# A hybrid decoder block on one NeuronCore: group-norm spread by a diagonal tile, row sums on 64 columns, one gate projection drawn forward, and a changed ending

## Chip, cores and metric

The kernel runs on one core of a Trainium2 chip. The metric is device time in microseconds (us) of one execution. PE is TensorE (PEld its weight loads), DVE VectorE, ACT ScalarE, POOL GpSimd, SP the engine that issues the DMAs.

## What is computed

One decoder block on a sequence of 1024 tokens and 1024 channels, in float32:

```python
h = modulate(rmsnorm(x, norm1_g), shift1, scale1)
u, v, val, gate = split(h @ w_in + b_in)                 # 512 channels each
y_a = gelu(u) * (causal_spatial(layernorm(gelu(v))) + b_s)   # 8 heads, chunks of 128 tokens
y_b = silu(groupnorm(conv31(val * sigmoid(gate)) + conv_b))  # 8 groups of 64 channels
x = x + gate1 * (concat(rmsnorm(y_a), rmsnorm(y_b)) @ w_out)
h2 = modulate(rmsnorm(x, norm2_g), shift2, scale2)
g, up = split(h2 @ w_ffn_in)                             # 2816 channels each
x = x + gate2 * ((silu(g) * up) @ w_ffn_out)
out = modulate(rmsnorm(x, norm_f_g), shift_f, scale_f)
```

The shifts, scales and gates are `silu(c) @ ada_w`, one vector each.

## The kernel before

Channels lie on partitions, tokens on the free axis; the 1024 tokens are worked as two halves of 512 (`half` 0 and 1). Each float32 product is made of three fp32r matmuls, 128x128 weights on 128x512 data: the data and the weights are each split into a rounded part (`wh_`, or the first plane of a tile, made by ACT) and the remainder (`wl_`, or the second plane, made by POOL or DVE), and `mm3` (L682 to L684) sums high*high, low*high, high*low in PSUM. In the feed-forward part the same is line 1073.

The stages stand in the program like this: first norm; value and gate projections `vg_proj` (`p` banks), which end in `glu` (ACT sigmoid, one DVE operation) and write `ypad`; `u_proj` (`pu`); `spatial_bias`; `v_proj` (`v`); the 31-tap convolution `conv`, almost all of it DVE operations on `cv` tiles (L1006); `group_norm`; `spatial` (`pm`); the norms of the two branches (`rstd`, `branch_out`), giving `y_a` and `y_b`; `w_out` (`po`); then the second norm, and the feed-forward part, of which the first quarter (`ah`) is interleaved with half 1 of the mixer. Raw weights come through a ring of four 128x1024 slots (`N_RAW = 4`, the tag "raw"), and so do the 64 columns of the conditioning matrix (`ada`), which DVE or POOL and ACT reduce in the background.

`group_norm` (L1021) works on a pair of 128-channel tiles. Two float32 matmuls with a centring matrix take the mean away (L1026); ACT squares; matmuls with 32 columns of weights collect the squares of both tiles in one 128x128 block, in which 32 partitions stand for one run of 128 tokens (L1033); ACT takes the root and DVE the reciprocal, `gsd` (L1036, L1037). Then the reciprocals are spread over all 128 partitions and 512 tokens. Half 1 (names `g10`, `g11` in `DIAGONAL`) does it by `diagonal` (L614): ACT rounds `gsd` to a high part `low`, four DVE operations on 32 partitions each (L620) write high or remainder into a 128x512 tile, block-diagonally and zero elsewhere, and one matmul per 128-channel tile with a 0/1 matrix `picks` spreads it (L1042). The tile is called `late`, and is made once, by `load_late`, after half 0 is done. Half 0 does it by blocks: 16 float32 matmuls per pair-half, 64 weight columns on 128x128 data, each a 0/1 column of `colt` (L1046). The norms of the branches have the same two ways (L733, L737).

`spatial_bias` (L786) sums the rows of the spatial weights `wt` of four heads at a time, by a float32 matmul of 128 equal columns (L789), and adds them to `bst` in eight DVE operations on 64 partitions (L794).

The last norm is worked in three pieces of the tokens (512, 256, 256). Sums of squares are matmuls with one column of data (L1345, bank `ssq_nf`); ACT and DVE give `rt_nf` (L1374, L1375); matmuls with the identity `eye` spread it (L1377); for each of eight tiles DVE multiplies (L1399), ACT adds the shift (L1401), and SP stores two tiles of 256 tokens at a time (L1403).

The order of the instructions is not that of the code: `fix_order` (L499) schedules the whole program on a list of modelled durations, forward and backward, and fixes each engine's order. Any edit can therefore move instructions on every engine.

Of the kernel before, what the change touches and what calls it, by code (L numbers as in the profile page):

```python
# [7 lines left out]
F32 = mybir.dt.float32  # L8
# [3 lines left out]
ALU = mybir.AluOpType  # L12
# [23 lines left out]
IDLE = (1, 1, 2, 3, 3)  # L36
BEFORE_LAST = ((3, 6), (2, 4), (3, 7), (3, 2))
# [11 lines left out]
    ("sel_grp", 16), ("low_rows", 1), ("sel_hl", 1),  # L49
# [466 lines left out]
def block_kernel(ctx: ExitStack, tc: tile.TileContext, xT, c, ada, cols, vbias, bs, wsp,  # L516
# [21 lines left out]
    def mm_bank(name):  # L538
        return ps.tile([P, 512], F32, tag="mm", name=name)
# [74 lines left out]
    def diagonal(src):  # L614

        diag, low = late["diag"], late["low"]
        A.activation(low, src, AF.Copy)
        for q in range(4):
            rows = slice(32 * q, 32 * q + 32)
            V.scalar_tensor_tensor(diag[rows, q * P:(q + 1) * P], low[rows].bitcast(F32), col("low_rows")[rows], src[rows],  # L620
                                   op0=ALU.mult, op1=ALU.add)
        return diag
# [163 lines left out]
    def spatial_bias():  # L786
        for q in range(2):
            rs = mm_bank(f"rs{q}")
            PE.matmul(rs, ones.broadcast_to([P, P]), wt[:, 4 * q:4 * q + 4, :], start=True, stop=True)  # L789
            for hh in range(4):  # L790
                hd = 4 * q + hh
                e, hp = hd % 2, hd // 2
                rows = slice(e * 64, (e + 1) * 64)
                V.scalar_tensor_tensor(bst[rows, hp, :], rs[rows, hh * P:(hh + 1) * P],  # L794
                                       col("a_ln_b", hp)[rows], bst[rows, hp, :],
                                       op0=ALU.mult, op1=ALU.add)
# [224 lines left out]
    def group_norm(half, jp, js, s):  # L1021
# [17 lines left out]
        both = sd if by_block else diagonal(sd)  # L1039
        for i, (j, b) in enumerate(zip(js, (b1, b0))):  # L1040
            if not by_block:
                PE.matmul(b, late["picks"][:, i * P:(i + 1) * P], both, start=True, stop=True)  # L1042
            for q in range(4):
                for g in range(2):
                    if by_block:
                        PE.matmul(b[g * 64:(g + 1) * 64, q * P:(q + 1) * P],  # L1046
                                  col("sel_grp", 8 * i + 2 * q + g).broadcast_to([P, 64]), sd,
                                  start=True, stop=True)
            V.tensor_tensor(s[j], s[j], b, op=ALU.mult)
            A.activation(s[j], s[j], AF.Silu, bias=col("b_gn_b", j), scale=col("b_gn_g", j))  # L1050
# [55 lines left out]
    background += [lambda i=i: ada_cols(SHIFT2 * 8 + i, pool=i < 12) for i in range(16)]  # L1106
    v_proj(0)
# [8 lines left out]
    vg_proj(1, (0, 1, 2))  # L1116
# [222 lines left out]
    sums, squares_in, norm_banks = {}, [0, 0, 0], {}  # L1339

    def to_partitions(i, t):

        part = pieces[i]
        for q in range((part.stop - part.start) // P):
            PE.matmul(norm_banks[i][:, q:q + 1], t[:, q * P:(q + 1) * P], ones,  # L1345
                      start=squares_in[i] == q == 0, stop=False, skip_group_check=True)
        squares_in[i] += 1
# [22 lines left out]
    def norm(i):  # L1370
        bank, part = norm_banks[i], pieces[i]
        nq = (part.stop - part.start) // P
# [7 lines left out]
    def output(i, tiles=range(KD), by_pool=()):  # L1380
# [6 lines left out]
        for k in tiles:  # L1387
# [10 lines left out]
            else:  # L1398
                V.scalar_tensor_tensor(t, x_tile(k, part), ccol(SCALEF, k), bank[:, 0:size],  # L1399
                                       op0=ALU.mult, op1=ALU.mult)  # L1400
                A.activation(t, t, AF.Identity, bias=ccol(SHIFTF, k))  # L1401
            if (k + 1) % per_store == 0:
                nc.sync.dma_start(out[(0, KD, KD + KD // 2)[i] + k // per_store], row)  # L1403
# [72 lines left out]
    with issue_after(last_ins):  # L1476
# [5 lines left out]
        norm_banks[1], norm_banks[2] = gn_bank("ssq_nf1"), mm_bank("ssq_nf2")  # L1482
        for i in (1, 2):
# [96 lines left out]
```

## Time and profile before

| | us |
|---|---|
| median of 3 runs (range) | 967.76 (966.22 to 967.87) |
| the profiled execution | 967.97 |
| its span, from first to last instruction | 965.9 |
| PE busy | 950.5 |
| DVE busy | 871.7 |
| ACT busy | 474.0 |
| POOL busy | 408.6 |

Rows of the timeline read: start, length, engine, line, operation, output<-inputs, weights' shape, form of the data, count; in brackets the idle time before them and what ended it. A float32 matmul leaves two or more records. Rows by tile read: shortest/median/longest in ns, first and last start. Rows by stretch give the length, then the busy time of PE, PEld, DVE, ACT and POOL, the granted TensorE clock (1.00 is full), and the DMA share and rate. Neighbouring matmuls overlap, so what one costs is read from start to start.

### The profile page before, as it was taken

Reading aid. Unit: us, or ns where it says so; the run is one execution under the profiler, and the core shown is the slowest. Engines: PE = TensorE matmul, PEld = TensorE weight load, DVE = VectorE, ACT = ScalarE, POOL = GpSimd, SP = SyncE. Lnnn points to the kernel's source line nnn. Section 1 sums busy time; section 2 is a strip of 40 time slices with the busy share of each in tenths; the row PEclk is TensorE's granted clock in tenths of the full one; section 3 lists DMA queues with packets and bytes.
Section 4 is the critical chain, followed back from the end, with each engine's and each line's share of the span. In section 5 each row is a group of like instructions: output and inputs, shape, how many; then the busy total and the mean of one; then the engine's idle time right before and its main releaser. Section 6 shows DMA issues by size and latency. Waiting matters only on the chain.

```text
span 965.9 us, 12960 instructions
## 1 busy us (share of the span) xinstructions
PE 950.5 (98%) x4521; PEld 769.6 (80%) x4521; DVE 871.7 (90%) x1236; ACT 474.0 (49%) x756; POOL 408.6 (42%) x241
## 2 busy tenths in 40 slices
PE   8999999999999999999999999999999999999996
PEld 4887777778777778788888888888888888888885
DVE  6999999999999763999999999999879999969956
ACT  5787477643474753564333333333337437227426
POOL 0089988836453413665444444455433100000132
PEclk9999999999999999999999999999999999999998
DMA  9882542343485444844677678867657857415104
GB/s 353 323 310 91 176 152 69 113 174 131 137 282 188 158 136 146 271 173 147 215 245 239 230 237 261 268 211 257 211 177 264 266 172 258 162 33 159 61 1 174
DMA packets 70498, 184.24 MB, mean 191 GB/s; under 512 B 7841, under 2 KB 8353, under 8 KB 70434
## 3 DMA queue, kind: packets, MB, share of 16 engines
q1 hardware_dynamic: 70434, 183.43, 56.5%
q8 instruction: 35, 0.57, 0.2%
q14 instruction: 29, 0.24, 0.1%
HBM read 142.24 MB, written 41.16 MB: 190 GB/s over the span
## 4 chain that ended last, share of the span: by engine, by line
PE 79%; DVE 15%; ACT 2%; DMA 2%; issue 1%; SPq 0%; ACTq 0%; DVEq 0%
PE B L1073 30%; PE C L1073 18%; PE ah L1073 10%; DVE cv L1006 5%; PE A L1073 3%; PE v L682 2%; PE v L684 2%; PE po L682 2%; PE po L684 2%; PE v L683 2%; PE po L683 2%; PE p L684 1%; PE p L683 1%; PE p L682 1%; DVE ada L636 1%
## 5 line engine op out<-in xcount | busy, mean ns | idle before, releaser
L1073 PE MATMUL B<-h,w_f 128*128 128x512 f32 x816 | 189.6, 389 | 0.1
L1073 PEld LDWEIGHTS B<-h,w_f 128*128 128x128 f32 x816 | 153.0, 188 | 32.5 <-ACT x L1291 0.8
L1006 DVE SCALAR_TENSOR_TENSOR cv<-ypad,colt,cv 128x512 f32<-128x512 f32 x216 | 147.0, 744 | 0.2
L1073 PE MATMUL B<-fa,w_d 128*128 128x512 f32 x528 | 124.8, 389 | 0.1
L1073 PE MATMUL C<-h,w_f 128*128 128x512 f32 x528 | 123.4, 389 | 0.0
L1073 PEld LDWEIGHTS B<-fa,w_d 128*128 128x128 f32 x528 | 98.8, 188 | 21.4 <-DVE x L1433 0.7
L1073 PEld LDWEIGHTS C<-h,w_f 128*128 128x128 f32 x528 | 99.1, 188 | 20.6
L1073 PE MATMUL ah<-h,wh_a 128*128 128x512 f32 x320 | 102.4, 396 | 0.3 <-ACT h L699 0.3
L1359 POOL TENSOR_TENSOR sq_nf<-sq_nf,sq_nf 128x512 f32<-128x512 f32 (+1 forms) x15 | 18.0, 1202 | 170.2 <-ACT sq_nf L1353 170.0
L666 POOL TENSOR_TENSOR wl_a<-raw_a,wh_a 128x1024 fp32r<-128x1024 f32 x20 | 49.8, 2488 | 78.2 <-ACT wh_a L665 78.2
L1065 ACT ACTIVATE w_d<-raw_d 128x512 fp32r<-128x512 f32 (+1 forms) x72 | 42.0, 593 | 80.9 <-PE B L1073 32.6
L1065 ACT ACTIVATE w_f<-raw_f 128x512 fp32r<-128x512 f32 x68 | 42.5, 629 | 75.9 <-PE B L1073 41.5
L1316 POOL TENSOR_TENSOR x<-x,up 128x512 f32<-128x512 f32 x20 | 33.2, 1659 | 105.6 <-ACT x L1315 105.6
L1066 DVE TENSOR_TENSOR w_f<-raw_f,w_f 128x512 fp32r<-128x512 f32 x68 | 70.2, 1039 | 2.6 <-ACT w_f L1065 2.5
L1073 PEld LDWEIGHTS ah<-h,wh_a 128*128 128x128 f32 x320 | 60.0, 188 | 15.7 <-ACT h L699 1.4
L1073 PE MATMUL C<-fa,w_d 128*128 128x512 f32 (+1 forms) x291 | 63.9, 370 | 0.0
L1073 PE MATMUL ah<-h,wl_a 128*128 128x512 f32 x160 | 62.5, 390 | 0.0
L1073 PEld LDWEIGHTS C<-fa,w_d 128*128 128x128 f32 x291 | 51.0, 188 | 9.2
L1066 DVE TENSOR_TENSOR fa<-a,fa 128x512 fp32r<-128x512 f32 x77 | 52.4, 720 | 0.4 <-ACT fa L1065 0.4
L1433 DVE SCALAR_TENSOR_TENSOR x<-B,cond,x 128x512 f32<-128x512 f32 x48 | 35.6, 745 | 18.2 <-PE B L1073 18.0
L1066 DVE TENSOR_TENSOR w_d<-raw_d,w_d 128x512 fp32r<-128x512 f32 (+1 forms) x72 | 49.1, 691 | 1.1 <-ACT w_d L1065 1.1
L1065 ACT ACTIVATE fa<-a 128x512 fp32r<-128x512 f32 x77 | 46.1, 625 | 7.1 <-DMA a<-acts 4.0
(265 smaller groups left out, 2111.2 us busy)
## 6 DMA issues: line engine op xcount, KB each, us to landing
acts<-x SPq DMA_DIRECT2D x77, 256.0 KB, 2.9
a<-acts SPq DMA_DIRECT2D x77, 256.0 KB, 4.0
raw_f<-wf SPq DMA_DIRECT2D x32, 512.0 KB, 4.0
ada<-ada SPq DMA_DIRECT2D x24, 512.0 KB, 3.5
x<-ada SPq DMA_DIRECT2D x24, 512.0 KB, 4.4
raw_a<-wf SPq DMA_DIRECT2D x20, 512.0 KB, 3.9
ahead<-ahead SPq DMA_DIRECT2D x40, 256.0 KB, 2.6
ypad<-ada SPq DMA_DIRECT2D x16, 512.0 KB, 5.7
```

Source lines behind the costliest of these rows:

```text
L636: V.scalar_tensor_tensor(raw, raw, 1.0, cact, op0=ALU.mult, op1=ALU.mult, accum_out=cond[:, j:j + 1])
L666: lo_eng.tensor_tensor(lo[:, cut], raw[:, cut], hi[:, cut].bitcast(F32), op=ALU.subtract)
L682: PE.matmul(acc, shi, mhi, start=start, stop=False)
L683: PE.matmul(acc, slo, mhi, start=False, stop=False)
L684: PE.matmul(acc, shi, mlo, start=False, stop=stop)
L1006: V.scalar_tensor_tensor(accs[j], src, wc, accs[j], op0=ALU.mult, op1=ALU.add)
L1065: A.activation(dst[:, 0, :], src, AF.Copy)
L1066: lo_eng.tensor_tensor(dst[:, 1, :], src, dst[:, 0, :].bitcast(F32), op=ALU.subtract)
L1073: last_mm = PE.matmul(bank[:, cols], s, m[:, cols], start=first and p == 0 and i == 0, stop=p == n - 1 and i == 2, skip_group_check=True)
L1316: G.tensor_tensor(g0, g0, up0, op=ALU.mult)
L1359: G.tensor_tensor(run, run, t, op=ALU.add)
L1433: V.scalar_tensor_tensor(x_tile(k, part), bank[:, cols], ccol(GATE2, k), x_tile(k, part), op0=ALU.mult, op1=ALU.add)
```

## The change

1. `group_norm` of half 0 spreads by `diagonal` too. Its tile `gd` takes one of the four raw slots for each of the two pairs: POOL clears the 128x512 part, ACT writes `picks` from four columns of `colt`; then ACT's copy, four DVE operations and two matmuls as in half 1.
2. `spatial_bias` sums even and odd heads by two matmuls of 64 columns, which lie beside each other in the array, into one bank, and adds them in four DVE operations on 128 partitions.
3. The gate and value projection of half 1, tile 0 (48 matmuls) is called ahead of `v_proj(0)`.
4. Ahead of the last spread, ten bf16 matmuls of 128x256 on `eye` go to a bank that nobody reads.
5. The shift of the very last tile is a DVE operation, and the last store is cut in two.

```diff
-    def diagonal(src):
-        diag, low = late["diag"], late["low"]
+    def diagonal(src, diag=None, low=None):
+        if diag is None:
+            diag, low = late["diag"], late["low"]
...
-        for q in range(2):
-            rs = mm_bank(f"rs{q}")
-            PE.matmul(rs, ones.broadcast_to([P, P]), wt[:, 4 * q:4 * q + 4, :], start=True, stop=True)
-            for hh in range(4):
...
-                V.scalar_tensor_tensor(bst[rows, hp, :], rs[rows, hh * P:(hh + 1) * P],
...
+        rs = mm_bank("rs")
+        heads = wt.rearrange("p (a e) t -> p e a t", e=2)
+        for e in range(2):
+            PE.matmul(rs[e * 64:(e + 1) * 64], ones.broadcast_to([P, 64]), heads[:, e], start=True, stop=True)
+        for hp in range(4):
+            V.scalar_tensor_tensor(bst[:, hp, :], rs[:, hp * P:(hp + 1) * P], col("a_ln_b", hp), bst[:, hp, :],
+                                   op0=ALU.mult, op1=ALU.add)
...
-        both = sd if by_block else diagonal(sd)
+        if by_block:
+            both = sb.tile([P, 2 * H], F32R, tag="raw", name=f"gd{half}{jp}", bufs=N_RAW)
+            diag, work = both[:, 0:H], both[:, H:]
+            G.memset(diag.bitcast(F32), 0.0)
+            picks = work[:, P:3 * P]
+            A.activation(picks.rearrange("p (a b) -> p a b", a=4), colt[:, _OFF["picks"]:_OFF["picks"] + 4].unsqueeze(2).broadcast_to([P, 4, 64]), AF.Copy)
+            both = diagonal(sd, diag, work[:, 0:P])
+        else:
+            picks, both = late["picks"], diagonal(sd)
         for i, (j, b) in enumerate(zip(js, (b1, b0))):
-            if not by_block:
-                PE.matmul(b, late["picks"][:, i * P:(i + 1) * P], both, start=True, stop=True)
-            for q in range(4):
-                for g in range(2):
-                    if by_block:
-                        PE.matmul(b[g * 64:(g + 1) * 64, q * P:(q + 1) * P],
-                                  col("sel_grp", 8 * i + 2 * q + g).broadcast_to([P, 64]), sd,
-                                  start=True, stop=True)
+            PE.matmul(b, picks[:, i * P:(i + 1) * P], both, start=True, stop=True)
...
+    vg_proj(1, (0,))
     v_proj(0)
...
-    vg_proj(1, (0, 1, 2))
+    vg_proj(1, (1, 2))
...
+IDLE_LAST = (0, 0, 10)
...
+        for _ in range(IDLE_LAST[i]):
+            ins = PE.matmul(idle_bank[:, 0:2 * P], eye.bitcast(BF16)[:, 0:P], eye.bitcast(BF16), start=True, stop=True).ins
+            edges.append((ins.name, sum_ins[i].name))
...
-                A.activation(t, t, AF.Identity, bias=ccol(SHIFTF, k))
-            if (k + 1) % per_store == 0:
-                nc.sync.dma_start(out[(0, KD, KD + KD // 2)[i] + k // per_store], row)
+                if i == 2 and k == KD - 1:
+                    V.tensor_scalar(t, t, ccol(SHIFTF, k), None, op0=ALU.add)
+                else:
+                    A.activation(t, t, AF.Identity, bias=ccol(SHIFTF, k))
+            store = out[(0, KD, KD + KD // 2)[i] + k // per_store]
+            if i == 2 and k >= KD - per_store:
+                cut = slice(k % per_store * size, (k % per_store + 1) * size)
+                nc.sync.dma_start(store[:, cut], t)
+            elif (k + 1) % per_store == 0:
+                nc.sync.dma_start(store, row)
```

The `edges` entry puts the fillers behind the last sum. The change of names in `_COLS` (16 columns `sel_grp` become 4 columns `picks`) goes with part 1.

The order on PE at the first spread of half 0, ahead and behind the change (`v_1` and `v_2` are the banks of the v projection; in both, neighbours on either side are of that projection). Before:

```order
L682 MATMUL v_1_1359<-wh_v_982,h_1_5_822 128x512
L683 MATMUL v_1_1359<-wh_v_982,h_1_5_822 128x512
L1046 MATMUL gn_1_1231<-gsd_0_1248,colt 64x128 x8
L1046 MATMUL gn_0_1230<-gsd_0_1248,colt 64x128 x8
L684 MATMUL v_1_1359<-wl_v_983,h_1_5_822 128x512
```

Now:

```order
L684 MATMUL v_2_1455<-wh_v_1030,h_1_1_798 128x512
L1049 MATMUL gn_1_1299<-gd_1319 128x512
L1049 MATMUL gn_0_1298<-gd_1319 128x512
L685 MATMUL v_2_1455<-wh_v_1030,h_1_1_798 128x512
L686 MATMUL v_2_1455<-wl_v_1031,h_1_1_798 128x512
```

Sixteen narrow matmuls have become two full ones, and they stand later within the v projection, which itself begins 48 matmuls later.

The order on PE in half 1, where `w_out` goes from the `y_a` products to the `y_b` products (`po_0` to `po_2` are the three banks open at that time, `ssq_b` is the spread of the branch's norm, on which `y_b` hangs). Before:

```order
L733 MATMUL ssq_b_3084<-late 128x512
L683 MATMUL po_2_3153<-y_a_1_2567,wl_o_2_3148 128x512
L684 MATMUL po_2_3153<-y_a_1_2567,wh_o_2_3147 128x512
L682 MATMUL po_2_3153<-y_a_2_2572,wh_o_2_3147 128x512
L683 MATMUL po_2_3153<-y_a_2_2572,wl_o_2_3148 128x512
L684 MATMUL po_2_3153<-y_a_2_2572,wh_o_2_3147 128x512
L682 MATMUL po_2_3153<-y_a_3_2577,wh_o_2_3147 128x512
L683 MATMUL po_2_3153<-y_a_3_2577,wl_o_2_3148 128x512
L684 MATMUL po_2_3153<-y_a_3_2577,wh_o_2_3147 128x512
L682 MATMUL po_0_3151<-y_b_0_3111,wh_o_0_3135 128x512
```

Now:

```order
L686 MATMUL po_2_3136<-y_a_2_2555,wh_o_2_3130 128x512
L735 MATMUL ssq_b_3067<-late 128x512
L684 MATMUL po_2_3136<-y_a_3_2560,wh_o_2_3130 128x512
L685 MATMUL po_2_3136<-y_a_3_2560,wl_o_2_3131 128x512
L686 MATMUL po_2_3136<-y_a_3_2560,wh_o_2_3130 128x512
L684 MATMUL po_0_3134<-y_b_0_3094,wh_o_0_3118 128x512
```

Eight products stood between the spread and the first reader of `y_b`; now three do.

The order on PE ahead of the `ah` products, at the spread of the second norm of half 0 (`ssq_n_0`; `p_3` are the two banks of the last gate projection of half 1). Before:

```order
L684 MATMUL p_3_2355<-h_1_1_798,wh_vg_3_2351 128x512
L682 MATMUL p_3_2355<-h_1_2_804,wh_vg_3_2351 128x512
L733 MATMUL ssq_n_0_2219<-late 128x512
L683 MATMUL p_3_2355<-h_1_2_804,wl_vg_3_2352 128x512
L684 MATMUL p_3_2355<-h_1_2_804,wh_vg_3_2351 128x512
```

Now:

```order
L684 MATMUL p_3_2307<-h_1_6_828,wh_vg_3_2303 128x512
L684 MATMUL p_3_2338<-h_1_0_792,wh_vg_3_2334 128x512
L735 MATMUL ssq_n_0_2202<-late 128x512
L685 MATMUL p_3_2338<-h_1_0_792,wl_vg_3_2335 128x512
L686 MATMUL p_3_2338<-h_1_0_792,wh_vg_3_2334 128x512
```

The spread has moved from the third to the first of the eight inputs of the last bank, and five products of the bank ahead (`p_3_2307`) have gone behind it: 17 matmuls stood between it and the first `ah` product, and 28 do now.

22 lines of the change are left out of this document (9 added, 13 removed).

## The prediction

> **What bounds the kernel now.** I read the page's busy shares and its chain first, then the busy time of each engine by stretch, then the PE and DVE rows at each place that the change touches.
>
> ```profile
> PE 950.5 (98%) x4521; PEld 769.6 (80%) x4521; DVE 871.7 (90%) x1236; ACT 474.0 (49%) x756; POOL 408.6 (42%) x241
> PE 79%; DVE 15%; ACT 2%; DMA 2%; issue 1%; SPq 0%; ACTq 0%; DVEq 0%
> 100.00:140.00 40.00, 40.00 (x183) 31.11 (x182) 39.82 (x68) 22.26 (x39) 35.13 (x17) 1.00 0.57 184
> 140.00:180.00 40.00, 40.00 (x305) 31.28 (x305) 39.54 (x57) 28.50 (x42) 31.92 (x20) 1.00 0.33 106
> 300.00:350.00 50.00, 49.73 (x243) 38.33 (x243) 38.66 (x60) 29.70 (x45) 17.11 (x10) 1.00 0.48 158
> 509.95 8.16 PE B L1073 x36
> ```
>
> PE is busy 98% of the span, and the chain of work is 79% PE and 15% DVE. In the stretch rows (length, then busy time of PE, PEld, DVE, ACT, POOL) PE is full between 100 and 180 us, where three of the five edits lie, so time taken off PE there shortens the program, unless another engine is then late. DVE is the one that could be: 39.8 and 39.5 of 40 us. It has slack again only after 300 (38.7 of 50). The last row gives the unit of account: 36 matmuls of 512 columns in 8.16 us, a **slot of 0.227 us**.
>
> **Group-norm spread (part 1).** The two spreads of half 0, on PE:
>
> ```profile
> 144.06 0.39 PE L683 MATMUL v<-wh_v,h 128*128 128x512 f32 x1
> 144.38 1.97 PE L1046 MATMUL gn<-gsd,colt 128*64 128x128 f32 x32
> 146.28 0.50 PE L684 MATMUL v<-wl_v,h 128*128 128x512 f32 x1
> 146.62 0.40 PE L682 MATMUL v<-wh_v,h 128*128 128x512 f32 x1
> ...
> 174.64 0.39 PE L683 MATMUL p<-h,wl_vg 128*128 128x512 f32 x1
> 174.96 1.09 PE L1046 MATMUL gn<-gsd,colt 128*64 128x128 f32 x16
> 175.98 1.16 PE L737 MATMUL ssq_a<-rt_a,sel_tok 128*128 128x128 f32 x8
> 177.07 1.09 PE L1046 MATMUL gn<-gsd,colt 128*64 128x128 f32 x16
> 178.09 0.50 PE L684 MATMUL p<-h,wh_vg 128*128 128x512 f32 x1
> L620 DVE SCALAR_TENSOR_TENSOR late<-late,colt,gsd x8: 327/344/1291, 316.7 to 332.4; 32x128 fp32r<-32x128 f32 x8
> L794 DVE SCALAR_TENSOR_TENSOR bst<-rs,colt,bst x8: 334/350/357, 112.5 to 115.1; 64x128 f32<-64x128 f32 x8
> ```
>
> From start to start, the first spread puts 146.28 - 144.06 - 0.227 = 1.99 us between two slots, and the slot after it takes 0.34 in place of 0.227: 2.11 us in all. Two full matmuls take 2 x 0.227 = 0.45, so 1.65 goes. The second: 178.09 - 174.64 - 0.227 = 3.22, of which ssq_a between the blocks is 177.07 - 175.98 = 1.09 and stays; 2.13 - 0.45 = 1.68. Together **-3.3 us** on PE. The cost moves to DVE: two spreads of four 32-partition pieces, 8 x 0.344 = 2.75 us (median of the same operation in half 1); part 2 gives back four of eight 64-partition pieces, 4 x 0.35 = 1.4. DVE is +1.35 us before 180, where it has under 0.7 us idle in 80; on PE this counts only where PE waits for DVE, taken up below. The ACT copies and POOL memsets fall on engines that are 57 to 88% busy there. I take -3.3, between -3.7 and -2.9: the long slots beside the blocks (0.34 in place of 0.227, twice in each spread) may go entirely, or stay.
>
> **Row sums on 64 columns (part 2).**
>
> ```profile
> 107.41 0.39 PE L684 MATMUL pu<-h,wh_u 128*128 128x512 f32 x1
> 107.63 1.88 PE L789 MATMUL rs<-wt,ones 128*128 128x512 f32 x4
> 109.29 0.50 PE L682 MATMUL v<-wh_v,h 128*128 128x512 f32 x1
> 109.63 0.39 PE L683 MATMUL v<-wh_v,h 128*128 128x512 f32 x1
> ```
>
> Four records take 1.66 us (107.63 to 109.29), 1.77 with the long slot behind them. Whether two 64-column tiles run side by side is told by the spread above: 32 records of 64 columns in 1.9 us is 59 ns a record, where ssq_a, 128 columns wide, takes 1.09 / 8 = 136 ns. So they do, and the four take 0.83 us, plus 0.2 for entering and leaving the narrow shape (0.32 + 0.34 - 2 x 0.227 at 144): **-0.7 us**; if they ran one after another, +0.1. Elsewhere the new order has one narrow block more than before (two sums of squares are split, one pair of others merged): **+0.2**. The Trainium skill (TensorEngine Tiling (Array Packing), Key Properties) says that a change of tiling mode drains TensorE; the trace bears it out with these 0.2 us. By a drain that eats the 0.83 saved, part 2 would be worth nothing and the sum 0.7 us higher.
>
> **Gate projection moved up (part 3).** Its 48 matmuls are only placed elsewhere; weights and queue entries (SP loads, POOL's and ACT's rounding) move with it, and an ACT table load that it adds early is saved later. What changes is which waits PE meets, in the new order:
>
> ```profile
> 267.83 0.80 PE L1073 MATMUL ah<-h,wh_a 128*128 128x512 f32 x1
> 268.47 0.40 PE L1073 MATMUL ah<-h,wl_a 128*128 128x512 f32 x1
> 270.94 0.50 PE L1073 MATMUL ah<-h,wh_a 128*128 128x512 f32 x1 [0.30 <-ACT h L699]
> 347.04 0.40 PE L733 MATMUL ssq_b<-late 128*128 128x512 f32 x1
> 349.10 0.41 PE L682 MATMUL po<-y_b,wh_o 128*128 128x512 f32 x1
> 348.32 1.95 ACT L964 ACTIVATE y_b<-yn_b 128x512 fp32r<-128x512 f32 x3 [3.89 <-DVE yn_b L962]
> ```
>
> (a) At the first ah products PE loses 268.47 - 267.83 - 0.227 = 0.41 and 0.30 waiting for h, which hangs on the spread of ssq_n_0. That stands 17 matmuls ahead of them, and 28 in the new order: 2.5 us more cover, so **-0.7**. (b) In half 1 the first product that reads y_b begins 2.06 us after ssq_b's spread, with nothing to spare: ACT makes y_b from 348.32, 0.65 each, so until 348.97. Eight matmuls lie between; in the new order three, 0.9 us, and all other work of the three open banks is done by then. So a **wait of 2.06 - 0.91 = +1.15** takes the place of work (0 if the chain before it comes earlier than PE does, up to 2 with DVE's +1.35 in front of it). (c) The vb remainder goes ahead of h_0_7 on DVE, into an idle 1.0 us; cost 0, bound +0.3.
>
> **The end (parts 4 and 5).**
>
> ```profile
> 954.26 0.60 PE L1377 MATMUL ssq_nf<-eye,rt_nf 128*128 128x128 f32 x4
> 954.89 1.16 PE L1345 MATMUL ssq_nf<-ones,sq_nf 128*128 128x1 f32 x8
> 957.33 0.16 DVE L1375 RECIPROCAL rt_nf<-rt_nf 128x2 f32<-128x2 f32 x1
> 957.54 1.23 PE L1377 MATMUL ssq_nf<-eye,rt_nf 128*128 128x128 f32 x4 [1.49 <-DVE rt_nf L1375]
> 958.88 3.22 DVE L1399 SCALAR_TENSOR_TENSOR of<-x,cond,ssq_nf 128x256 f32<-128x256 f32 x8 [0.62 <-PE ssq_nf L1377]
> 959.39 3.34 ACT L1401 ACTIVATE of<-of,cond 128x256 f32<-128x256 f32 x8 [0.46 <-DVE of L1399]
> 957.00:958.00 1.00, 0.46 (x2) 0.46 (x3) 1.00 (x5) 1.00 (x3) 0.00 (x0) 0.54 0.68 262
> 953.37 1.07 PE C L1073 x8
> ```
>
> The last spread takes 1.23 us, the one before it, alike, 0.60; the granted clock fell to 0.54 in that microsecond, after 1.49 us without PE work. Ten fillers of 256 columns at 1.07 / 8 = 0.134 (estimate from the last row) fill 956.05 to 957.39, before the reciprocal ends at 957.49. If the clock then holds, **-0.63**; at half clock the fillers would end at 958.73 and put the spread off by 1.2. The Trainium skill (TensorE: Matmul & The Clock Gate, Part 1) has the clock halve after an idle window of some 3.4 us; here it was halved after 1.49 us, so the trace differs. By that rule the fillers would change nothing and the sum be 0.63 higher. Last shift: ACT's eight take 0.417 each and end at 962.73. Seven end at 962.31; DVE is free at 962.10 and would do the eighth by 962.5 at 0.40. SP issues one store more; I take **-0.2**, between -0.5 and +0.2.
>
> **Sum.** -3.3 - 0.7 + 0.2 - 0.7 + 1.15 - 0.63 - 0.2 = -4.2 us. The profiled execution took 967.97 us, 2.1 more than its span of 965.9 and 0.2 over the median of 967.76. So 967.97 - 4.2 = **963.8 us**.
>
> **Rivals.** (A) The change does not do all it says: column tiles follow one another (+0.8) and the clock drops in spite of the fillers (+0.63): 965.2. Against it is the 59 ns record; for it, that the clock fell with PE busy shortly before. (B) **DVE becomes the bound, and it is slower than before.** Eight vn shifts now have other neighbours:
>
> ```profile
> L921 DVE TENSOR_SCALAR vn<-vn,mv,sd x8: 541/1512/2620, 141.3 to 176.8; 128x512 f32<-128x512 f32 x8
> 202.59 0.66 PE L737 MATMUL ssq_b<-rt_b,sel_tok 128*128 128x128 f32 x4
> 206.45 3.06 DVE L965 TENSOR_TENSOR y_b<-yn_b,y_b 128x512 fp32r<-128x512 f32 x3
> 210.09 0.68 DVE L965 TENSOR_TENSOR y_b<-yn_b,y_b 128x512 fp32r<-128x512 f32 x1
> ```
>
> They take 0.54 to 2.62 us for one shape, the long ones while POOL works. From half 0's ssq_b spread to its last y_b DVE needs 210.77 - 202.59 = 8.2 us; in the new order PE reaches that product's remainder 34 matmuls and the spread itself later, about 8.6, so under 1 us is spare, and what makes DVE late makes PE late. DVE's operations ahead of it add up to some 4 us more than before at that point, since work was drawn forward, and PE comes 3 to 4 us sooner. Were all eight shifts 2.62 in place of a mean 1.4, DVE would be 10 us later, PE 9: 972.8. Below 5.2 us of delay (1 spare, 4.2 gained) the result is still not slower. For it: DVE is the fullest engine beside PE. Against it: POOL has no more work there than two memsets. (C) The same coupling, small: one to three shifts longer, 1 to 4 us lost, 964.8 to 967.8.
>
> **How the numbers follow.** Forecast as it stands, with its terms' own bounds (962 to 965): 0.50. A: 0.14. C: 0.22. B: 0.09. Better than 962, with no wait at y_b and a shorter tail: 0.05. The range of 8 in 10 goes from 961.8 to 967.8: it leaves out B and the ends of C and of the better case. A measurement of this kernel tells about 0.2% (1.9 us) from no change. Faster by more than that is under 965.8: forecast, better, nearly all of A and a third of C, 0.75. Within it: the rest of C and the lower end of B, 0.17. Slower: 0.08.
>
> **What would show it.** Spreads: gn<-gd rows of two matmuls with 0.45 us from the slot ahead to the slot behind. Row sums: rs in about 1 us. Waits: the ah products without gaps over 0.1 us, and a PE wait of about 1.1 us at half 1's first y_b product. End: the last spread at 0.6 us with the granted clock at 1.00. I am wrong if PE's idle time between 140 and 240 us is over 1 us, or if y_b's wait in half 0 or 1 is over 2.

## The result and the profile after

| | before | after |
|---|---|---|
| median (range), 4 runs each, same chip | 967.30 us (966.22 to 967.87) | 971.84 us (971.44 to 972.91) |
| ratio to before, 95% interval | 1 | 1.0050 (1.0038 to 1.0062) |
| the profiled execution | 967.97 us | 971.91 us |
| its span | 965.9 us | 969.9 us |

The change makes the kernel **slower by about 0.5%**, where 963.8 us, a gain of 4.2, had been forecast. The profiled executions differ by +3.9 us. Most of the rows show what was forecast of them; the time is lost in waits that the sum didn't hold. Two disturbed runs further down, one of 1596 us (`change_less_vector`) and one of 5446 us (`change_psum_less_vector`), are left out of the medians and ratios.

Busy time of the engines, from the page of the kernel after:

```profile
PE 948.3 (98%) x4470; PEld 766.7 (79%) x4471; DVE 879.9 (91%) x1241; ACT 473.8 (49%) x759; POOL 409.4 (42%) x243
```

PE is busy 2.2 us less (950.5 before), and the span is 4.0 longer: PE stands still 21.6 us in place of 15.4. DVE is busy 8.2 us longer. By stretch (length, then PE, PEld, DVE, ACT, POOL), after:

```profile
140.00:180.00 40.00, 40.00 (x242) 29.46 (x241) 38.85 (x54) 30.30 (x49) 30.93 (x19) 1.00 0.28 93
180.00:220.00 40.00, 35.52 (x220) 28.12 (x219) 39.92 (x51) 18.96 (x26) 22.27 (x12) 1.00 0.43 149
300.00:350.00 50.00, 48.78 (x233) 36.13 (x232) 44.38 (x66) 29.89 (x45) 17.13 (x10) 1.00 0.47 153
```

And the stretch of before that the prediction didn't show:

```profile
180.00:220.00 40.00, 40.00 (x220) 31.71 (x217) 39.92 (x51) 17.87 (x24) 21.61 (x12) 1.00 0.36 122
```

Between 180 and 220 us PE went from no idle time to 4.48 us, while DVE has next to none in either kernel. From 300 to 350 us DVE is busier than before (38.66 there): 31 of the convolution's operations with `ypad` and `cv` as inputs start in that stretch, and 21 did before. The waits of PE after, summed between 20 and 950 us (us in total, times, longest):

```profile
PE pm L946 <- DVE s L1050: 1.7, 1, 1.7
PE ssq_b L739 <- DVE rt_b L733: 1.4, 1, 1.4
PE B L1074 <- ACT x L1293: 1.0, 1, 1.0
PE po L684 <- ACT y_b L963: 0.9, 1, 0.9
PE ssq_a L739 <- DVE rt_a L733: 0.9, 1, 0.9
PE gn L1049 <- DVE late L622: 0.8, 1, 0.8
...
PE gn L1049 <- DVE gd L622: 0.5, 1, 0.5
```

Its eleven lines sum to 8.9 us. The same view of before has 1.7 us in four lines, the longest this:

```profile
PE ssq_n L737 <- DVE rt_n L731: 1.0, 1, 1.0
```

Four of the new waits (`s`, `rt_b`, `rt_a`, `gd`: 1.7 + 1.4 + 0.9 + 0.5 = 4.5 us) are the whole loss of that stretch, and each is a wait for DVE. `gd` and `s` (2.2 us) lie on the path of the second pair's spread. `rt_a` and `rt_b` (2.3 us) are the reciprocals of the branches' norms, which come late because of what stands ahead of them in DVE's order. DVE there, after (start, length, engine, line, operation, count):

```profile
181.56 0.94 DVE L1036 RECIPROCAL gsd<-gsd 128x128 f32<-128x128 f32 x1
...
185.29 1.41 DVE L622 SCALAR_TENSOR_TENSOR gd<-gd,colt,gsd 32x128 fp32r<-32x128 f32 x4
186.73 2.72 DVE L920 TENSOR_SCALAR vn<-vn,mv,sd 128x512 f32<-128x512 f32 x1
189.38 0.73 DVE L961 SCALAR_TENSOR_TENSOR yn_a<-ya,colt,ssq_a 128x512 f32<-128x512 f32 x1
190.04 1.27 DVE L1050 TENSOR_TENSOR s<-s,gn 128x512 f32<-128x512 f32 x2
```

GpSimd beside them:

```profile
186.78 2.39 POOL L668 TENSOR_TENSOR wl_o<-raw_o,wh_o 128x1024 fp32r<-128x1024 f32 x1 [3.38 <-ACT wh_o L667]
```

Left out in the middle are a `vn` shift of 1.27 us, the reciprocal `rt_a` behind it (183.61) and two more `vn` shifts. From the reciprocal to the multiplication `s`, which uses the spread and for which TensorE's next narrow products `pm` wait, 8.5 us pass. Before it was 3.3, with `rt_a` and one `vn` shift between:

```profile
172.85 0.94 DVE L1037 RECIPROCAL gsd<-gsd 128x128 f32<-128x128 f32 x1
...
174.53 1.62 DVE L921 TENSOR_SCALAR vn<-vn,mv,sd 128x512 f32<-128x512 f32 x1
176.17 0.69 DVE L1049 TENSOR_TENSOR s<-s,gn 128x512 f32<-128x512 f32 x1
```

The four pieces take 1.41 of the 8.5. The `vn` shift behind them takes 2.72, about as long as GpSimd's 2.39 us product lasts; the shortest of the kernel before took 0.54.

The first pair's pieces, and GpSimd beside them:

```profile
151.31 5.31 DVE L622 SCALAR_TENSOR_TENSOR gd<-gd,colt,gsd 32x128 fp32r<-32x128 f32 x4
```

```profile
149.63 11.00 POOL L1000 TENSOR_TENSOR s<-s,cp 128x512 f32<-128x512 f32 x8
```

Those four pieces take 1.3 us each, the second four 0.34. PE doesn't wait for the first four: it is busy for all of 140 to 180 us. All eight cost 6.6 us of DVE where 2.75 had been put down:

```profile
L622 DVE SCALAR_TENSOR_TENSOR gd<-gd,colt,gsd 32x128 fp32r<-32x128 f32 x8 | 6.6, 828 | 0.1
```

Last, ahead of the reciprocal `rt_b`, on which half 0's `y_b` hangs, stand two `ada` sums, 3.4 us each:

```profile
204.98 3.41 DVE L638 SCALAR_TENSOR_TENSOR ada<-ada,cact 128x1024 f32<-128x1024 f32 x1
208.32 3.45 DVE L638 SCALAR_TENSOR_TENSOR ada<-ada,cact 128x1024 f32<-128x1024 f32 x1
213.09 0.94 DVE L733 RECIPROCAL rt_b<-rt_b 128x128 f32<-128x128 f32 x1
```

What came out as forecast, on PE: the two spreads, the row sums, the wait at half 1's first `y_b` product, and the end.

```profile
107.16 1.08 PE L792 MATMUL rs<-wt,ones 128*64 128x512 f32 x4
108.17 0.50 PE L684 MATMUL p<-h,wh_vg 128*128 128x512 f32 x1
...
187.55 0.39 PE L1049 MATMUL gn<-gd 128*128 128x512 f32 x1
187.78 0.40 PE L685 MATMUL p<-h,wl_vg 128*128 128x512 f32 x1
...
351.85 0.50 PE L684 MATMUL po<-y_b,wh_o 128*128 128x512 f32 x1 [0.88 <-ACT y_b L963]
...
960.43 1.25 PE L1375 MATMUL idle_end<-eye 128*128 128x256 bf16 x10
962.06 0.71 PE L1382 MATMUL ssq_nf<-eye,rt_nf 128*128 128x128 f32 x4 [0.37 <-DVE rt_nf L1380]
```

A spread product takes one slot (187.78 - 187.55 = 0.23). The row sums take 1.01 us from start to start (1.66 before). The last spread takes 0.71 in place of 1.23, and the granted clock stays at 1.00 over it; whether the fillers did that is taken up with `only_end`.

**The account**, for the two profiled executions. Narrow blocks are the runs of short or narrow products between two full ones; the centring products, the row sums and the new spread products are counted with them here. Between 60 and 216 us, from the slot ahead of each block to the slot behind it, less one slot, they take 25.1 us before (17 blocks) and 25.3 after (21). Waits of 1.0 before and of 0.88 + 0.53 + 1.68 + 1.40 = 4.5 after lie inside them, so the work fell by 24.1 - 20.8 = 3.3; 3.8 had been forecast. The end gave 0.6 (from the last sums to the last instruction 11.0, then 10.4). All of PE's waits together grew by 8.9 - 1.7 = 7.2, and 4.5 of that are the four waits on DVE. That is -3.3 - 0.6 + 7.2 = +3.3 of the 4.0 by which the span grew; the remaining 0.7 was not traced.

### The profile page after: what moved, and what is told of

It is laid out like the page before. It is cut to its first block, busy times and chain, and to the rows that moved or that the text cites. A ratio compares the mean times of both kernels' runs of the same rounds, so it can differ in the third digit from the quotient of the medians.

```text
span 969.9 us, 12863 instructions
## 1 busy us (share of the span) xinstructions
PE 948.3 (98%) x4470; PEld 766.7 (79%) x4471; DVE 879.9 (91%) x1241; ACT 473.8 (49%) x759; POOL 409.4 (42%) x243
## 4 chain that ended last, share of the span: by engine, by line
PE 78%; DVE 13%; DMA 4%; ACT 2%; issue 2%; SPq 0%; POOL 0%; DVEq 0%; POOLq 0%; ACTq 0%
PE B L1074 29%; PE C L1074 16%; PE ah L1074 8%; PE po L686 3%; PE po L684 3%; PE po L685 3%; PE A L1074 3%; PE pu L684 2%; PE pu L686 2%; PE pu L685 2%; DVE cv L1005 1%; PE v L686 1%; PE v L685 1%; PE v L684 1%; DVE ada L638 1%
```

## The experiments

All kernels compute the whole block; `unused_pieces`, `held_slots`, `unused_pieces_own` and `pieces_only` only add work that nothing reads. Ratios are to the kernel before on the same chip, with their 95% interval.

| kernel | median, us | ratio (interval) |
|---|---|---|
| only_spread | 977.13 | 1.0101 (1.0087 to 1.0115) |
| only_gate | 969.79 | 1.0025 (1.0015 to 1.0034) |
| only_rowsums | 969.04 | 1.0016 (1.0008 to 1.0025) |
| only_end | 967.39 | 0.9996 (0.9985 to 1.0006) |
| without_gate | 981.20 | 1.0136 (1.0113 to 1.0159) |
| without_spread | 968.42 | 1.0014 (1.0006 to 1.0023) |
| spread_from_psum | 971.02 | 1.0037 (1.0024 to 1.0050) |
| only_spread_from_psum | 972.28 | 1.0053 (1.0039 to 1.0066) |
| unused_pieces | 984.55 | 1.0174 (1.0155 to 1.0192) |
| change_less_vector | 967.86 | 1.0002 (0.9991 to 1.0014) |
| before_less_vector | 970.89 | 1.0031 (1.0020 to 1.0041) |
| change_psum_less_vector | 972.74 | 1.0053 (1.0036 to 1.0070) |
| held_slots | 968.62 | 1.0012 (1.0001 to 1.0023) |
| unused_pieces_own | 985.55 | 1.0192 (1.0178 to 1.0205) |
| before_three_tmp | 984.19 | 1.0174 (1.0161 to 1.0187) |
| only_spread_own | 987.86 | 1.0218 (1.0202 to 1.0233) |
| pieces_only | 985.81 | 1.0206 (1.0191 to 1.0220) |
| change_one_tile | 971.75 | 1.0053 (1.0038 to 1.0067) |

### Each part alone

The theories: the loss comes from the spread's new work on VectorE; or from the gate projection's new place; or from the order that the scheduler makes of all parts together. Four kernels put one part of the change on the kernel before: the spread (with its raw slots),

```diff
+            both = sb.tile([P, 2 * H], F32R, tag="raw", name=f"gd{half}{jp}", bufs=N_RAW)
...
+            PE.matmul(b, picks[:, i * P:(i + 1) * P], both, start=True, stop=True)
```

> The kernel before with part 1 alone (half 0 of the group norm spread by a diagonal tile). Theory S, the spread on VectorE is what costs: the first four VectorE pieces took 5.31 us in place of 1.4 in the changed kernel, VectorE falls behind and TensorE waits for it between 140 and 220 us; time 968.5 to 970.5, with over 3 us of TensorE waits there. Theory V, the gate projection drawn forward is what costs, since it puts v, the group norm and the branch norm 10 us later on TensorE and w_out sooner: this kernel has no such move, so it keeps the 3.3 us that TensorE is spared, 963.5 to 965.

the gate projection,

```diff
+    vg_proj(1, (0,))
     v_proj(0)
...
-    vg_proj(1, (0, 1, 2))
+    vg_proj(1, (1, 2))
```

> The kernel before with part 3 alone (gate projection of half 1, tile 0, ahead of v_proj(0)). Theory V: 970 to 972, with 3 to 5 us of TensorE waits between 140 and 220 us, at the branch norms and at the first products that read y_b. Theory S: 966.5 to 968, no new wait over 1 us.

the row sums,

```diff
+            PE.matmul(rs[e * 64:(e + 1) * 64], ones.broadcast_to([P, 64]), heads[:, e], start=True, stop=True)
```

> The kernel before with part 2 alone (row sums on 64 columns). TensorE is spared 0.7 us and VectorE 1.4: 966.6 by theories S and V. Its order in the feed-forward part is another one than before's, as in the changed kernel. Theory F, that the two waits of 0.6 and 1.1 us in the feed-forward part of the changed kernel come from that other order: 967.5 to 968.5, with waits of the same kind after 440 us.

and the end, parts 4 and 5.

```diff
+IDLE_LAST = (0, 0, 10)
...
+                    V.tensor_scalar(t, t, ccol(SHIFTF, k), None, op0=ALU.add)
```

> The kernel before with parts 4 and 5 alone (ten fillers ahead of the last spread, last shift on VectorE, last store in two). All theories: the last spread takes 0.6 to 0.7 us at full clock in place of 1.23, and the end comes 0.5 us sooner, 966.8; if the fillers do nothing by themselves and the clock only happened to hold in the changed kernel, 967.2.

No part alone is faster. The spread costs 9.9 us, the gate 2.5, the row sums 1.8; the end's 0.1 is within the noise. They sum to +14 against +4.5 for all together: **the parts don't add**. The waits of PE with the spread alone, from 140 to 220 us:

```profile
PE pm L949 <- DVE mx L953: 3.6, 3, 2.4
PE gn L1028 <- DVE s L1017: 1.8, 1, 1.8
PE pm L949 <- DVE s L1053: 1.4, 2, 1.1
```

The longest are on DVE again, though behind other operations than in the whole change. The spread alone is over 6 us slower than the slowest time expected of it (970.5). With the gate's move alone PE has no such wait between 140 and 220 us, which speaks against the theory of the gate's new place, and the time still lies between the two that were expected. In the row sums' case the 0.65 us appears in its row and is lost again: 21 narrow blocks in place of 17 (split `gsq` and `pm` blocks) do the same 24.1 us of work, with 2.2 us of waits in place of 1.0. Between 440 and 950 us no wait of PE is listed there, so the feed-forward order isn't the reason.

With the end alone the last spread takes 0.71 us, as in the whole change. But it can do so without the fillers. The kernel with the gate alone has none, PE stands still for 1.49 us as before, and the clock is 1.00 (its last spread, then the stretch of 0.70 us from its start):

```profile
959.72 0.71 PE L1383 MATMUL ssq_nf<-eye,rt_nf 128*128 128x128 f32 x4 [1.49 <-DVE rt_nf L1381]
959.72:960.42 0.70, 0.70 (x4) 0.52 (x4) 0.70 (x2) 0.70 (x3) 0.00 (x0) 1.00 0.63 240
```

Of the twelve kernels here without fillers, nine took 0.71 us in their profiled execution and three 1.22 to 1.23 at a clock of 0.50 (the kernel before, `only_spread_from_psum`, `only_spread_own`), all after the same 1.49 us. All eight with fillers took 0.71. So the kernel before was profiled in the rarer case, and eight executions don't settle whether the fillers prevent it. Where the clock held, the old ending mostly takes 10.5 us from the last sums on, and the new one 10.4 to 10.5.

### The whole change without one part

```diff
-    vg_proj(1, (0,))
-    vg_proj(1, (1, 2))
+    vg_proj(1, (0, 1, 2))
```

> The changed kernel without part 3 (parts 1, 2, 4 and 5). Part 1 alone gave 977.1 and the whole change 971.8, so something in the whole makes up for 5 us. Theory I, the gate projection drawn forward does: it gives TensorE 48 matmuls that wait for nothing while the spread's chain runs on VectorE. Then 974 to 976.5 here, with 6 us or more of TensorE waits between 140 and 220 us. Rival, the row sums (1.4 us less on VectorE) and chance do, and the gate move costs its 2.5 us here as well: 968 to 970.5.

```diff
-            both = diagonal(sd, diag, work[:, 0:P])
+        both = sd if by_block else diagonal(sd)
```

> The changed kernel without part 1 (parts 2 to 5). Theory S, the spread on VectorE is the one part that loses time in the whole: 966 to 968.5, little of it waits between 140 and 220 us. Rival A, the parts' losses add up (2.5 for the gate, 1.8 for the row sums): 971.

Without the gate's move the kernel is some 13 us slower than before: the move isn't the loser, it makes up for 8 to 9 us of what the other parts cost. That is more than was expected of it (974 to 976.5 us). PE stands still for 11 us there, 9.8 of it at the same four waits (`rt_b` 4.3, `s` 2.3, `gd` 2.2, `rt_a` 1.0), and the granted clock falls to 0.83:

```profile
180.00:220.00 40.00, 28.99 (x169) 22.39 (x168) 38.10 (x47) 19.29 (x27) 20.03 (x12) 0.83 0.40 132
```

Without the spread the waits are gone and DVE has slack:

```profile
180.00:220.00 40.00, 40.00 (x263) 31.99 (x262) 36.86 (x50) 20.86 (x27) 22.42 (x12) 1.00 0.37 120
```

This is what was expected if the spread is the part that loses: in the company of the other parts it is worth +3.4 us, where -3.3 had been forecast.

### Pieces that GpSimd can't hold up

The pieces read two SBUF operands. Here the reciprocals stay in PSUM, in the whole change and with the spread alone:

```diff
-        sd = sb.tile([P, P], F32, tag="rt", name=f"gsd{half}_{jp}", bufs=2)
+        sd = b0[:, P:2 * P] if f"g{half}{jp}" not in DIAGONAL else sb.tile([P, P], F32, tag="rt", name=f"gsd{half}_{jp}", bufs=2)
```

> The changed kernel with the reciprocals of half 0 kept in PSUM (the bank of the sums, next 128 columns), so that the four VectorE pieces of a spread read one operand from SBUF and not two. In the traces so far these pieces take 0.34 us where GpSimd is idle and 1.3 to 1.7 where it works; operations that read one operand from PSUM take 0.74 either way. Theory S, that these stalls of the spread are what loses the time: pieces of 0.35 us in all places, 8 pieces in 2.8 us and not 6.6, and 966 to 968.5 us. Rival O, that it is the order (what stands in which place), and the stalls are only beside it: pieces short, and 970.5 to 973.

> Part 1 alone, with the reciprocals in PSUM as well. Theory S: pieces of 0.35 us; 977.1 comes down by 4 us or more, to 973 or less. Rival O: 975.5 to 978, with TensorE still waiting 6 us or more between 140 and 220 us.

DVE's groups between 100 and 220 us with the reciprocals in PSUM, whole change:

```profile
L638 DVE SCALAR_TENSOR_TENSOR ada<-ada,cact 128x1024 f32<-128x1024 f32 x5 | 16.4, 3272 | 0.7 <-POOL sq_a L726 0.7
L622 DVE SCALAR_TENSOR_TENSOR gd<-gd,colt,gn 32x128 fp32r<-32x128 f32 x8 | 2.7, 342 | 0.1
```

and the changed kernel's `ada` there:

```profile
L638 DVE SCALAR_TENSOR_TENSOR ada<-ada,cact 128x1024 f32<-128x1024 f32 x5 | 10.6, 2129 | 0.0
```

The eight pieces fall from 6.6 to 2.7 us. In the two kernels all sixteen take 0.33 to 0.36 us, twelve of them beside a working GpSimd. Alone, the spread improves by some 4.7 us, as expected if the pieces' stalls are what costs. The whole change improves by only about 1 (medians 0.8, ratios 1.3, with intervals that overlap), as expected if it is the order. There a `vn` shift of 2.47 us stands between the pieces and `s` again, with 1.5 us of wait at `pm`, and the five `ada` sums take 5.8 us more. Most of that has nothing to do with the time saved, since one sum grew from 1.21 to 6.08 us beside GpSimd long before the first piece, which runs at 155.5:

```profile
101.73 6.08 DVE L638 SCALAR_TENSOR_TENSOR ada<-ada,cact 128x1024 f32<-128x1024 f32 x1
```

The edit moved it there, and so this experiment isn't a clean one either.

### Less work on VectorE

Four of the `ada` columns that VectorE shares go to GpSimd and ScalarE, in the changed kernel, in the kernel before, and together with the reciprocals in PSUM:

```diff
-    background += [lambda i=i: ada_cols(SHIFT2 * 8 + i, pool=i < 12) for i in range(16)]
+    background += [lambda i=i: ada_cols(SHIFT2 * 8 + i, pool=True) for i in range(16)]
```

> The changed kernel with the last four of the 16 background columns of the conditioning matrix reduced by GpSimd and ACT, as the other 12 are, and no longer by VectorE (four operations of 1.2 to 3.4 us, two of them right ahead of the reciprocal that TensorE waits for at 213 us). Theory L: 967 to 969.5. Rival C: 971 to 973, since the chain from the sums to the spread is as long as before.

> The same four columns moved off VectorE in the kernel before. Theory L, with VectorE just keeping up there: no gain to speak of, 966 to 967.5, TensorE being full already. Rival N, that VectorE bounds the kernel before as well: 964 to 965.5.

> The changed kernel with the reciprocals in PSUM and the four columns moved off VectorE: VectorE is about 10 us lighter than in the changed kernel. Theory L: the TensorE time that the change spares comes to light, 964 to 966.5, under the kernel before. Rival C: 970 to 972.

The changed kernel gains some 4 us (medians 4.0, ratios 4.6) and is level with before, as expected if VectorE's load is what costs. The kernel before loses 2.8 by the same edit, which neither theory expected; this load wasn't what held it. Changed kernel with less on VectorE, PE by stretch, and DVE at the second pair:

```profile
180.00:220.00 40.00, 39.50 (x234) 30.61 (x233) 39.92 (x52) 25.92 (x40) 34.30 (x18) 1.00 0.51 162
```

```profile
181.10 0.92 DVE L1036 RECIPROCAL gsd<-gsd 128x128 f32<-128x128 f32 x1
181.94 6.12 DVE L920 TENSOR_SCALAR vn<-vn,mv,sd 128x512 f32<-128x512 f32 x3
...
188.84 2.69 DVE L622 SCALAR_TENSOR_TENSOR gd<-gd,colt,gsd 32x128 fp32r<-32x128 f32 x4
...
192.69 1.27 DVE L1050 TENSOR_TENSOR s<-s,gn 128x512 f32<-128x512 f32 x2
```

This corrects the theory: from reciprocal to `s` it is 11.6 us here, longer than the 8.5 of the changed kernel, and PE doesn't wait for it, because more full products stand ahead of the spread in this order: from the last sums of squares to the first `gn<-gd` PE works through for 13.3 us (178.4 to 191.7), while the changed kernel has 9.0 us of work there and 1.4 of waits (176.4 to 186.75). Behind the pieces the one `vn` shift takes 0.55 us here, 2.72 there. **Between these two kernels, not the length of the path decides, but the work of PE that is planned beside it.** The two remedies together (972.74) are no better than the change itself, where a time under the kernel before was expected; the waits then sit elsewhere (2.6 us at a feed-forward product, 1.9 for `sg`).

### Load, slots or path

Pieces that nobody reads, beside the old spread, with the raw slot (`unused_pieces`); slots held and cleared but no pieces (`held_slots`):

```diff
+            gd = sb.tile([P, 2 * H], F32R, tag="raw", name=f"gd{half}{jp}", bufs=N_RAW)
+            diagonal(sd, gd[:, 0:H], gd[:, H:H + P])
```

> The kernel before, which still spreads by blocks, with the diagonal tile of part 1 made as well (ACT's copy and four VectorE pieces per spread, and the raw slot), but read by nobody. TensorE's work is that of before. Theory L, load: VectorE is as full as TensorE there, and 2.8 us of pieces plus their stalls delay what TensorE waits for: 970 to 974. Rival C, chain: the pieces cost because they stand between the reciprocal and the spread, and the normalised tile comes late; here nothing waits for them, so 966.5 to 968.5.

```diff
+            G.memset(gd[:, 0:H].bitcast(F32), 0.0)
+            A.activation(gd[:, H:H + P], sd, AF.Copy)
```

> The kernel before, with two raw slots held as part 1 holds them (cleared by GpSimd when the slot comes free, written once more by ACT after the reciprocal, read by nobody), and not one VectorE piece. Theory R, the raw slots: in the kernels with part 1 the gate projection's weights are issued late (the third load of raw_vg at 162.6 us in the kernel with part 1 alone, the first at 158.4 with the unused pieces, against 133.0 and 122.0 before), and TensorE runs out of work that waits for nothing. Then 972 to 985 here. Theory L, load on VectorE: 966.5 to 968.5.

The first can't be read as meant, since its slot is written for the first time at 145.8 us, and the loads behind it in the ring had to wait: the gate weights' first load goes out at 158.4 us, before at 122.0 (shortest/median/longest ns, first and last start; the kernel with unused pieces, then before):

```profile
L659 SPq DMA_DIRECT2D raw_vg<-wvg x8: 327/328/382, 158.4 to 243.0; - x8
```

```profile
L658 SPq DMA_DIRECT2D raw_vg<-wvg x8: 328/328/328, 122.0 to 226.9; - x8
```

Its 16 us can thus not be put down to the pieces. Slots alone, cleared early as in the change, cost 1.4 us, which the runs barely resolve and which is far from the some 5 us or more expected if the slots were the loss. It goes by a readable path: an `ada` sum in DVE's queue waits for its load, and `s` stands behind it, and PE waits 1.9 us for `s`.

```profile
180.06 1.23 DVE L636 SCALAR_TENSOR_TENSOR ada<-ada,cact 128x1024 f32<-128x1024 f32 x1 [2.52 <-DMA ada<-ada]
```

To be rid of the slot, a buffer of its own was made room for by dropping two of five temporaries, with the pieces unused, with nothing else as a control, and with the spread in use:

```diff
-N_TMP = 5
+N_TMP = 3
...
+            gd = front.tile([P, 2 * H], F32R, tag="gd", name=f"gd{half}{jp}", bufs=1)
```

> The unused pieces again, now in a buffer of their own (room made by three temporary tiles in place of five), so that all four raw slots carry loads. Theory R: most of the 16.5 us goes, 967 to 971. Theory L: 976 or more.

> Control for the two kernels with a buffer of their own: the kernel before with three temporary tiles in place of five and nothing else. All theories: what the missing room costs, 967 to 971; the others are read against this one.

> Part 1 alone with the diagonal tile in a buffer of its own (three temporary tiles). Theory R: TensorE keeps its 3.3 us, less what the VectorE pieces cost, so from 2 us under the control to 1 above it. Theory L: 5 us or more above the control, as 977.1 is 9.9 above the kernel before.

The control alone costs 17 us, so little can be told from these three: over it the unused pieces cost 1.4 us, within the intervals, and the spread 3.7. The last try keeps all temporaries and writes the eight pieces to a small scratch tile:

```diff
+            scr = front.tile([P, P], F32R, tag="scr", name=f"scr{half}{jp}", bufs=1)
+            for q in range(4):
+                rows = slice(32 * q, 32 * q + 32)
+                V.scalar_tensor_tensor(scr[rows], sd[rows], col("low_rows")[rows], sd[rows], op0=ALU.mult, op1=ALU.add)
```

> The kernel before with eight pieces of 32x128 on VectorE (four a pair of heads, at the place where the change makes its spread, written to a small scratch tile that nothing reads) and nothing else: no GpSimd clearing, no ScalarE pattern, no raw slot, TensorE's spread as before. The planner is told of them. Theory L (the load of the pieces on VectorE, 3 to 7 us in the window from 140 to 190 us, is what costs): 969.5 to 973, with TensorE waiting 2 us or more between 140 and 220 us. Theory P (the pieces cost only because the group norm's product waits for them, reciprocal to pieces to product): no wait hangs on them here, 966.5 to 968.5.

It costs 19 us, far more than either theory allowed. The first row sums start at 112.88 us (107.63 before), so 5.2 us are gone **before the first piece runs**, at 152.1. DVE of that kernel, then of before:

```profile
80.91 2.12 DVE L636 SCALAR_TENSOR_TENSOR ada<-ada,cact 128x1024 f32<-128x1024 f32 x1
...
83.62 0.94 DVE L731 RECIPROCAL rt_n<-rt_n 128x128 f32<-128x128 f32 x1
```

```profile
76.61 0.94 DVE L731 RECIPROCAL rt_n<-rt_n 128x128 f32<-128x128 f32 x1
```

The scheduler has drawn `ada` and `cv` work ahead of the first norm's reciprocal, which comes 7 us later. So the load of the pieces can't be priced by adding it: the order answers, and by more than the load.

### A version meant to beat both

One spread tile for both pairs, in one slot, and the four `ada` columns off VectorE:

```diff
+            first = "gd" not in late
+            if first:
+                late["gd"] = sb.tile([P, 2 * H], F32R, tag="raw", name="gd", bufs=N_RAW)
+            both = late["gd"]
```

> The changed kernel with one spread tile for both pairs of heads (one raw slot, cleared and given its pattern once, the diagonal pieces written anew for the second pair) and, as in change_less_vector, the four ada columns that VectorE still shared left to GpSimd and ScalarE. Theory S (VectorE's chain at the second pair and the slots that the tiles hold are what the change loses by): 965.5 to 968, below the kernel before if the second pair's pieces do not wait for the first pair's product. If the one tile brings a wait in its place (the second pair's pieces cannot be written before TensorE has read the first's): 969 to 972, with gd as the releaser of PE at the second pair.

It isn't faster. PE waits 0.3 us for `gd`, so neither of the two expected ways came true. The longest wait is for ScalarE's `sg`, which starts at 202.14, behind an `ada` sum that it was given and a table load:

```profile
202.88 0.50 PE L684 MATMUL p<-h,wh_vg 128*128 128x512 f32 x1 [2.52 <-ACT sg L758]
```

```profile
199.68 1.06 ACT L636 ACTIVATE ada<-ada 128x1024 f32<-128x1024 f32 x1 [0.89 <-POOL ada L635]
...
200.84 1.28 ACT L758 ACT_TABLE_LOAD   x1
```

No version here beats the kernel before.

## Why the prediction was wrong

**Part 1, the step that failed.** "The cost moves to DVE ... 8 x 0.344 = 2.75 us", which "counts only where PE waits for DVE, taken up below". PE's saving came nearly as forecast (3.3 of 3.8 us with the row sums). But "below" only `y_b` was taken up. The waits were nearer. The pieces lie between the reciprocal and `s`, for which `pm` waits, with whatever `vn` and `yn_a` work the order puts between, and the reciprocals `rt_a` and `rt_b` stand in the same order behind `vn` and `ada` work. Those places had no term at all. Measured there: 4.5 us of waits on DVE in 180 to 220 us, 2.2 for `gd` and `s` and 2.3 for `rt_a` and `rt_b`, against a line that called over 1 us the sign of being wrong. The price was too low as well: it was a median of half 1, where seven of eight pieces ran beside an idle GpSimd. In half 0 the first four ran beside a working one, and the eight took 6.6 us; the same row of the trace had 1291 ns as its longest. It looks like the smaller error, since PE doesn't wait for the first four, and with all eight at 2.7 us the whole change was still at 971.02 us; but that kernel had another order, so this isn't shown. The Trainium skill (SBUF — State Buffer, Who interferes with whom) says that a VectorE instruction with two SBUF inputs contends with a GpSimd instruction that reads SBUF. The traces agree: 1.3 us in place of 0.34 for a piece beside GpSimd's products, and 0.33 to 0.36 with one input in PSUM.

**Rival B** named the mechanism (a `vn` shift beside POOL, 2.62 us) and was given 0.09. It came true at 186.73 with 2.72 us, but behind the pieces rather than at `y_b`, and without all eight being long: their sum fell from 10.7 to 9.4 us in 100 to 220. The argument against it, that POOL got no more work, missed that a long shift's place counts. So B's 972.8 lies near the measured 971.84 by chance. Rival C, the same coupling held to 1 to 4 us, was right in kind and too short in size.

**Rows that held.** Row sums: from the slot ahead to the slot behind 1.88 us before (107.41 to 109.29) and 1.33 after (106.84 to 108.17), so -0.55 (forecast -0.7). The forecast put 0.2 us down to entering and leaving the narrow shape; but the long slot behind, 0.11 of it, stands behind the full-width row sums of the kernel before too (109.29 to 109.63), so at most the rest can be the price of a change of shape. The `ah` products: no gaps where before 0.41 and 0.30 stood. Half 1's `y_b`: 0.88 us idle, 1.04 from start to start over a slot (forecast 1.15).

**A term that held by luck.** The last spread took 0.71 us at clock 1.00 with 0.37 of idle ahead of it (forecast 0.6 at 1.00). But the -0.63 was the difference from one execution of the kernel before, in which the clock had fallen. In nine of the twelve executions without fillers it held over the same 1.49 us, and there the new end, -0.83 in the sum, is worth about 0.05. By the Trainium skill's rule of an idle window of some 3.4 us (TensorE: Matmul & The Clock Gate, Part 1) the fillers would change nothing. Those nine traces agree with it; the three others had half the clock after 1.49 us, and why isn't known here.

**What the sum lacked.** Terms were added as if each part moved only its own instructions. The single parts give +9.9, +2.5, +1.8 and 0, all of them together +4.5. The prediction read three places of the new order and priced DVE by its total. Beside the four waits on DVE the others grew by 7.2 - 4.5 = 2.7 us net: 0.9 at half 1's `y_b`, which had a term, and the rest at places that no term named (`late`, `sg`, `ahead`, feed-forward `x`). Waits of about a microsecond at a feed-forward product turn up, at other places each time, also in kernels that keep the feed-forward order of before (1.1 us with the slots held, 0.9 with the end alone), so they aren't put down to that order.

**Shown and open.** Shown: the loss in 180 to 220 us is PE waiting for DVE; undoing the spread, or taking `ada` columns off VectorE, removes those waits and 3.4 to 4.6 us. Shown too: the path's length alone doesn't do it (11.6 us without such a wait), and the gate's move isn't the loser in the whole change. Open: how much of the loss is VectorE's time and how much the order that the scheduler happened to find, since every edit that was meant to separate the two (a scratch tile, a buffer, a column moved) reordered the program, by 1 to 19 us.

## What to carry to other kernels

Where the engine that gets the work is as full as the one that is relieved, price the work at its duration beside the neighbours that it will have there, and follow the new instruction from what feeds it to who waits for it, not only its total. A saving on the bound engine is kept only where its own planned work covers that path. In a program ordered by a scheduler, small gains don't add: compare the whole, and take a control for each edit that is meant to change nothing. A term read off one execution of the kernel before is a guess until a second execution shows the same.

## What the runs showed of the hardware

A VectorE piece of 32x128 with both operands in SBUF took 0.34 us, and 1.29 to 1.38 beside GpSimd's products in the changed kernel, at most 2.57 (the spread alone); with one operand in PSUM all sixteen took 0.33 to 0.36, twelve of them beside GpSimd's products. A 128x1024 sum with two operands in SBUF took 1.21 us with GpSimd idle, and up to 6.08 beside it.

After 1.49 us without TensorE work near the end, the granted clock at the next products was 1.00 in nine profiled executions and 0.50 in three, which took 1.22 to 1.23 us for what the nine did in 0.71.
